# Two MLP steps on unsplit float32 operands, and pools that wait tile by tile

## The chip, the cores and the metric

The kernel runs on one core of a Trainium2 chip. The metric is the device time of one execution in microseconds (us). Times of instructions come from one execution that the hardware profiler recorded; it counts them from the start of its span.

## The reference

One layer of an encoder on x of 2048 rows by 1024, float32, in three parts: a norm and an input projection; two mixers (mLSTM heads and a Hyena convolution), whose outputs are gated, normed and go through one output projection with a norm and a residual; and an MLP. The change touches the end of the second part and the start of the third:

```
mix = concat(y_m, y_h) @ w_out                 # 2048x1024 @ 1024x1024
x   = x + rms_norm(mix, norm_mix_post)
hm  = rms_norm(x, norm_mlp_pre)
ff  = square(relu(hm @ w_mlp_in)) @ w_mlp_out  # 1024 -> 4096 -> 1024
x   = x + rms_norm(ff, norm_mlp_post)
```

## The kernel before

**Products.** Most matrix products are made of *split* operands: `split` (lines 166 and 169) rounds a tile to float32r on ScalarE (`hi`, a CAST) and subtracts it from the source on VectorE or GpSimd (`lo`). `mm3` then issues three matmuls, lo by hi, hi by lo and hi by hi (lines 159 to 161). Given an operand that is not a pair, it issues one plain float32 matmul.

**The MLP's first product** is a seven-product scheme on 2x2 blocks. Step s (0 to 31) takes 128 of 2048 paired output columns (s % 16) for one half of the rows (s // 16). `up_step` makes the products 1, 2, 6, 5, 7, 4, 3 in this order, each over k = 0 to 3 with 128x512 outputs in a bank of PSUM, and after each adds on VectorE, then relu and square on ScalarE, then stores of the results to `ga`. Product i needs a right operand `hm[i]` (1 MB, made of transposed rows and kept for sixteen steps) and a weight made by `up_weights`: two loads of 512 KB (`raw`, whose quarters are a11, a21, a12, a22), sums and differences on GpSimd (`s12`), and splits of all of it on ScalarE and GpSimd into seven tiles `cb`. `right_load` fetches an operand from DRAM (`ht`) into the space of its `lo` part, as two DMAs; `right_split` splits it in place, half by half.

**Order around step 0.** `out_proj` works through 16 blocks of 128 rows in a loop over i. For block i it transposes gated rows (`turned`), multiplies them with the output weights (`part`, four calls, into two banks `po`), and `finish` and `normed` make the residual row and its norm; `turn_out` of an earlier block transposes the normed rows and, for odd blocks, forms the seven operands on GpSimd and writes them to `ht`. In i = 11 to 14 a generator, `first_operands`, loads and splits right operands 1 and 2 and the weights of step 0. In i = 15 to 17 `first_step` runs step 0 in pieces between the last rows. In this loop the instructions of TensorE, VectorE and ScalarE keep the written order (`manual_schedule`); SP's and GpSimd's queues, and all queues in the MLP, are ordered by a planner. Banks for `po` come from a pool of three (`pp`); two more (`h1p`) serve block 1 and products 1, 2, 5 and 7 of step 0. Later steps take turns in eight banks.

**Order around step 16.** In step 15 the space of each right operand is read for the last time, and its load for the second half of the rows is issued behind that product; the split follows two products later:

```python
            if s == 15:
                self.right_load(1, i)
                loaded.append(i)
            if len(loaded) > (2 if s == 15 else 0):
                j = loaded.pop(0)
                self.right_split(j, pool if j in (2, 7, 3) else None)
```

Weights of step s + 2 are loaded, and those of s + 1 are prepared, after product 2 of step s; their raw tiles rotate through six buffers, three a step. Loads are issued from SP (line 231), most stores from ScalarE (line 234).

Of the kernel before, what the change touches and what calls it, by code (L numbers as in the profile page):

```python
# [8 lines left out]
F32 = mybir.dt.float32  # L9
F32R = mybir.dt.float32r  # L10
AF = mybir.ActivationFunctionType
ALU = mybir.AluOpType
# [135 lines left out]
class Builder:  # L148
# [95 lines left out]
    def build(self):  # L244
        tc, nc = self.tc, self.nc
        with ExitStack() as c:
            cp = c.enter_context(tc.tile_pool(name="cp", bufs=1))
# [24 lines left out]
            with ExitStack() as c2:  # L272
                self.pw = pj.enter_context(tc.tile_pool(name="pwk", bufs=2, reuse_waits="tile"))
                self.pp = pj.enter_context(tc.tile_pool(name="pps", bufs=4, space=PSUM))
# [7 lines left out]
            gp = c.enter_context(tc.tile_pool(name="gp", bufs=1, side="right"))  # L282
# [6 lines left out]
            for i, n in enumerate(("mlstm_norm_w", "hyena_norm_w")):  # L289
# [3 lines left out]
                   hy.enter_context(tc.tile_pool(name="hps", bufs=3, space=PSUM, side="right")))  # L293
# [7 lines left out]
            op = self.op = late.enter_context(tc.tile_pool(name="opre", bufs=1, side="right"))  # L301
# [3 lines left out]
            self.mtail = late.enter_context(tc.tile_pool(name="mtail", bufs=2, side="right"))  # L305
            self.mwk = ms.enter_context(tc.tile_pool(name="mwk", bufs=2, reuse_waits="tile"))
            self.mps = ms.enter_context(tc.tile_pool(name="mps", bufs=5, space=PSUM))
# [3 lines left out]
            self.h1p = c.enter_context(tc.tile_pool(name="h1p", bufs=2, space=PSUM))  # L311
            oc = ExitStack()
            self.hq = c.enter_context(tc.tile_pool(name="hmq", bufs=1))
# [6 lines left out]
            hp = c.enter_context(tc.tile_pool(name="hmp", bufs=1, side="right"))  # L320
            self.hm_pool.update({i: hp for i in (1, 2)})
            self.hm = {}
            self.cb = c.enter_context(tc.tile_pool(name="cb", bufs=1, side="right"))
# [10 lines left out]
    def long_conv(self, pools, hy, early):  # L334
# [3 lines left out]
        self.mearly = early.enter_context(self.tc.tile_pool(name="mearly", bufs=1, side="right"))  # L338
        self.mpk = early.enter_context(ExitStack())
        self.mps0 = self.mpk.enter_context(self.tc.tile_pool(name="mps0", bufs=1, space=PSUM, side="right"))  # L340
# [10 lines left out]
    def filters(self, c, consts):  # L351
        tc = self.tc
        kp = c.enter_context(tc.tile_pool(name="kp", bufs=1, side="right"))
        wk = c.enter_context(tc.tile_pool(name="kwk", bufs=2, side="right"))
        ps = c.enter_context(tc.tile_pool(name="kps", bufs=2, space=PSUM, side="right"))
        yield from self.filter_net(kp, wk, ps, consts)
        yield from self.filter_spectra(kp, wk, ps, c.enter_context(tc.tile_pool(name="kmps", bufs=1, space=PSUM, side="right")))

    def filter_loads(self, c):

        tc, io, pool = self.tc, self.io, self.pool
        kp = c.enter_context(tc.tile_pool(name="kc", bufs=1, side="right"))
# [956 lines left out]
    def out_proj(self, c):  # L1319
# [134 lines left out]
        for i in range(18):  # L1454
# [41 lines left out]
            if 10 < i < 15:  # L1496
                next(staged)
# [454 lines left out]
```

## Time and profile before

| | |
|---|---|
| time, median of 3 runs | 2719.76 us (2715.68 to 2721.2) |
| the profiled execution's own time | 2723.08 us |
| its span | 2721.3 us |
| mean granted clock of TensorE | 0.983 |
| busy: TensorE, VectorE, ScalarE, GpSimd | 96%, 56%, 45%, 45% |

PE is TensorE's matmuls, PEld its weight loads, DVE is VectorE, ACT ScalarE, POOL GpSimd, SP the engine that issues most loads; a q behind a name is the engine's queue of instructions. A matmul's record is longer than the distance to the next one, since they overlap. In rows of waits, `PE po L159 <- DVE xo` reads: TensorE's instruction of line 159 for tile po waited for VectorE's on xo. The clock is given as a share of full speed (2.4 GHz; the other level is 1.2 GHz).

### The profile page before, as it was taken

Reading aid. Unit: us, or ns where it says so; the run is one execution under the profiler, and the core shown is the slowest. Engines: PE = TensorE matmul, PEld = TensorE weight load, DVE = VectorE, ACT = ScalarE, POOL = GpSimd, SP = SyncE. Lnnn points to the kernel's source line nnn. Section 1 sums busy time; section 2 is a strip of 40 time slices with the busy share of each in tenths; the row PEclk is TensorE's granted clock in tenths of the full one; section 3 lists DMA queues with packets and bytes.
Section 4 is the critical chain, followed back from the end, with each engine's and each line's share of the span. In section 5 each row is a group of like instructions: output and inputs, shape, how many; then the busy total and the mean of one; then the engine's idle time right before and its main releaser. Section 6 shows DMA issues by size and latency. Waiting matters only on the chain.

```text
span 2721.3 us, 35529 instructions
## 1 busy us (share of the span) xinstructions
PE 2602.7 (96%) x12293; PEld 2125.3 (78%) x12293; DVE 1527.1 (56%) x2453; ACT 1237.2 (45%) x2300; POOL 1220.3 (45%) x973
## 2 busy tenths in 40 slices
PE   6999999999999998889997999989999999999998
PEld 4778888777798887767775888868888888888876
DVE  5676653777547666656455444464444433544478
ACT  6355544555544446643334454454444333222244
POOL 1211114555235443446676877677772340311232
PEclk8999999999999999989998999989999999999999
DMA  6233346665676549556755444554446453444546
GB/s 172 61 87 113 112 124 215 191 190 175 215 234 185 181 154 297 152 158 222 231 177 200 171 138 166 181 185 150 148 163 254 164 181 108 121 146 159 186 161 218
DMA packets 288355, 465.76 MB, mean 171 GB/s; under 512 B 37542, under 2 KB 149414, under 8 KB 287152
## 3 DMA queue, kind: packets, MB, share of 16 engines
q1 hardware_dynamic: 227600, 324.85, 38.3%
q10 hardware_dynamic: 53264, 117.53, 11.4%
q0 software_dynamic: 7312, 21.11, 3.1%
q8 instruction: 98, 1.61, 0.3%
q14 instruction: 81, 0.66, 0.1%
HBM read 289.27 MB, written 174.13 MB: 170 GB/s over the span
## 4 chain that ended last, share of the span: by engine, by line
PE 40%; DVE 5%; POOL 3%; DMA 3%; ACT 2%; issue 2%; ACTq 0%; DVEq 0%; POOLq 0%; SPq 0%
PE pm L160 13%; PE pm L161 13%; PE pm L159 13%; DVE cb L169 1%; POOL xt L1255 1%; DVE hm L169 1%; ACT xo L1393 1%; DMA m<-ga 1%; DVE hm L1877 0%; DMA m<-in_w_mlp_out_dram 0%; POOL cb L169 0%; DMA hm<-ht 0%; DVE xo L1396 0%; POOL ht L1428 0%; DVE hm L1807 0%
## 5 line engine op out<-in xcount | busy, mean ns | idle before, releaser
L166 ACT CAST cb<-m 128x1024 fp32r<-128x1024 f32 (+1 forms) x346 | 281.2, 847 | 442.6 <-PE pm L159 387.5
L169 DVE TENSOR_TENSOR cb<-m,cb 128x1024 fp32r<-128x1024 f32 (+1 forms) x222 | 232.5, 1084 | 306.0 <-ACT cb L166 296.3
L160 PE MATMUL pm<-hm,cb 128*128 128x512 f32 x896 | 354.6, 396 | 18.4 <-DVE hm L169 13.2
L159 PE MATMUL pm<-hm,cb 128*128 128x512 f32 x896 | 354.1, 396 | 11.1 <-POOL cb L169 6.2
L161 PE MATMUL pm<-hm,cb 128*128 128x512 f32 x896 | 352.8, 394 | 0.0
L160 PE MATMUL pm<-cb 128*128 128x512 f32 x880 | 343.4, 390 | 7.8 <-DVE cb L169 7.8
L159 PE MATMUL pm<-cb 128*128 128x512 f32 x880 | 342.3, 389 | 1.0 <-DVE cb L169 1.0
L161 PE MATMUL pm<-cb 128*128 128x512 f32 x880 | 342.5, 389 | 0.0
L169 POOL TENSOR_TENSOR cb<-m,cb 128x1024 fp32r<-128x1024 f32 x124 | 270.7, 2196 | 71.6 <-ACT cb L166 71.6
L1689 DVE TENSOR_TENSOR m<-pm,m 128x512 f32<-128x512 f32 x224 | 154.2, 690 | 250.8 <-PE pm L161 224.7
L159 PE MATMUL pt<-hn,w 128*128 128x512 f32 x640 | 270.1, 422 | 1.7 <-ACT hn L486 1.6
L160 PE MATMUL pt<-hn,w 128*128 128x512 f32 x640 | 254.2, 397 | 0.3 <-DVE hn L487 0.2
L161 PE MATMUL pt<-hn,w 128*128 128x512 f32 x640 | 253.3, 396 | 0.0
L169 POOL TENSOR_TENSOR raw<-raw,hi 128x512 fp32r<-128x512 f32 x160 | 206.1, 1300 | 100.6 <-ACT hi L166 75.4
L160 PEld LDWEIGHTS pm<-hm,cb 128*128 128x128 f32 x896 | 170.5, 190 | 59.3 <-DVE hm L169 16.6
L159 PEld LDWEIGHTS pm<-hm,cb 128*128 128x128 f32 x896 | 170.6, 190 | 51.0 <-POOL cb L169 7.9
L160 PEld LDWEIGHTS pm<-cb 128*128 128x128 f32 x880 | 165.1, 188 | 45.9 <-DVE cb L169 11.8
L161 PEld LDWEIGHTS pm<-hm,cb 128*128 128x128 f32 x896 | 170.4, 190 | 36.1
L159 PEld LDWEIGHTS pm<-cb 128*128 128x128 f32 x880 | 165.1, 188 | 35.9 <-ACT junk L1862 1.4
L161 PEld LDWEIGHTS pm<-cb 128*128 128x128 f32 x880 | 165.2, 188 | 34.0
L1693 ACT ACTIVATE m<-m 128x512 f32<-128x512 f32 x128 | 80.5, 630 | 220.4 <-DVE m L1689 213.1
L635 POOL DMA_DIRECT2D vp<-vst x96 | 61.3, 642 | 232.0 <-ACT vst L631 230.9
(322 smaller groups left out, 5672.0 us busy)
## 6 DMA issues: line engine op xcount, KB each, us to landing
ga<-m ACTq DMA_DIRECT2D x96, 512.0 KB, 4.4
m<-ga SPq DMA_DIRECT2D x96, 512.0 KB, 3.8
d<-st ACTq DMA_DIRECT2D x64, 512.0 KB, 3.0
m<-in_w_mlp_in_dram SPq DMA_DIRECT2D x62, 512.0 KB
m<-in_w_mlp_out_dram SPq DMA_DIRECT2D x114, 256.0 KB, 4.0
raw<-d SPq DMA_DIRECT2D x96, 256.0 KB, 3.2
xt<-in_x_dram SPq DMA_DIRECT2D x32, 512.0 KB, 4.0
dk<-kst SPq DMA_DIRECT2D x32, 512.0 KB, 3.8
```

Of the source, the lines that this page charges most:

```text
L159: pe.matmul(ps, w[1], x[0], start=first, stop=False)
L160: pe.matmul(ps, w[0], x[1], start=False, stop=False)
L161: pe.matmul(ps, w[0], x[0], start=False, stop=last)
L166: self.act.copy(hi, src)
L169: (eng_lo or self.dve).tensor_tensor(lo, src, hi.bitcast(F32), ALU.subtract)
L635: pool.dma_start(dst[:, 8 * b + e:8 * b + 8:2, cc:cc + 128], st[64 * e:64 * e + 64])
L1255: eng.tensor_tensor(res[:, cs], tmp[e], res[:, cs], ALU.add)
L1393: act.activation(x1, xt, AF.Square, accum_out=ss1[:, h:h + 1])
L1689: dve.tensor_tensor(dst, a, b, ALU.add)
L1693: act.activation(g, g, AF.Relu)
```

## The change

Steps 0 and 16 (the first of each half of the rows) make their products of plain float32 operands: the right operand as loaded, the weights as loaded or as summed. `up_weights(plain=True)` makes only the sums, and forms the weight of product 3 in place after product 2 has used the same space. The right operands are split behind the products: one after each later product (`split_held`), the last of them in the step that follows.

`first_operands` no longer runs in pieces: i = 11 and 12 only load operands 1 and 2, and the weights of step 0 are loaded when i = 14 ends, into a pool `m0` in place of the projection's scratch. Raw weights of step 1 go to free `cb` tiles. The norm of row 15 stands ahead of the third product of step 0. Weights of step 18 are loaded after product 3 of step 16, not after product 2.

The second output bank of each odd block up to 13 comes from `h1p`. And 25 pools are opened with `reuse_waits="tile"`: a tile in space that an earlier pool held waits for the tiles that lay there, where it waited for the release of that whole pool (`pwk`, `hwk`, `mwk`, `mmk` and some others had it already).

```diff
--- before.py
+++ after.py
-            cp = c.enter_context(tc.tile_pool(name="cp", bufs=1))
+            cp = c.enter_context(tc.tile_pool(name="cp", bufs=1, reuse_waits="tile"))
...
-            self.h1p = c.enter_context(tc.tile_pool(name="h1p", bufs=2, space=PSUM))
+            self.h1p = c.enter_context(tc.tile_pool(name="h1p", bufs=2, space=PSUM, reuse_waits="tile"))
...
-        def banks():
-            return [pp.tile([128, 512], F32, tag="po", name=f"po{e}", bufs=3) for e in range(2)]
+        def banks(i):
+
+            return [self.h1p.tile([128, 512], F32, tag="h1", name="po1") if e and i % 2 and i < 15 else
+                    pp.tile([128, 512], F32, tag="po", name=f"po{e}", bufs=3) for e in range(2)]
 
...
-        pos[0] = banks()
+        pos[0] = banks(0)
...
-        staged = self.first_operands(scratch)
-        wl = c.enter_context(tc.tile_pool(name="owl", bufs=2, side="right"))
+        wl = c.enter_context(tc.tile_pool(name="owl", bufs=2, side="right", reuse_waits="tile"))
...
-                    step = self.first_step(c, pp)
+                    step = self.first_step(pp)
                     next(step)
                     part(pos[i], 1, ym[i], 0)
                     next(step)
                     rows = finish(i, pos.pop(i))
+                    xns[i] = normed(i, *rows)
                     next(step)
-                    xns[i] = normed(i, *rows)
                 else:
                     next(step)
-            if 10 < i < 15:
-                next(staged)
+            if i in (11, 12):
+                self.right_load(0, i - 10)
             if i == 14:
                 gc.close()
+                self.first_operands(c)
             yield
         c.close()
 
...
-    def up_weights(self, s, raw, s12, pieces=False):
+    def up_weights(self, s, raw, s12, pieces=False, plain=False):
 
...
+        if plain:
+
+            pool.tensor_tensor(s12[:, 1], s12[:, 0], a11, ALU.subtract)
+            places = {1: a11, 7: a21, 2: a12, 4: a22, 5: s12[:, 0], 6: s12[:, 1], 3: a12}
+            yield lambda i, k: places[i][:, k, :]
+            pool.tensor_tensor(a12, a12, s12[:, 1], ALU.subtract)
+            yield
...
-    def first_operands(self, scratch):
-
-        for i in (1, 2):
-            self.right_load(0, i)
-        yield
-        self.right_split(1, self.pool)
-        yield
-        self.right_split(2, self.pool)
-        raw = [scratch("wr").rearrange("p (k f) -> p k f", k=4) for _ in range(2)]
-        g = self.up_weights(0, raw, scratch("ws").rearrange("p (i k f) -> p i k f", i=2, k=4))
-        next(g)
-        yield
-        self.w1_first = next(g)
-        yield
-
-    def first_step(self, c, pp):
-
-        wk = c.enter_context(self.tc.tile_pool(name="m0", bufs=1))
+    def first_operands(self, c):
+
+        m0 = self.m0 = c.enter_context(self.tc.tile_pool(name="m0", bufs=1))
+        raw = [m0.tile([128, 4, 256], F32, tag="r", name="m0", bufs=3) for _ in range(2)]
+        self.w_first = self.up_weights(0, raw, m0.tile([128, 2, 4, 128], F32, tag="r", name="m0", bufs=3), plain=True)
+        next(self.w_first)
+
+    def first_step(self, pp):
+
+
         count = [0]
+        self.held = []
 
         def tile(shape, tag):
-            return wk.tile(list(shape), F32, tag=tag, name="m0", bufs={"g": 3, "s": 1, "r": 3}[tag])
+            return self.m0.tile(list(shape), F32, tag=tag, name="m0", bufs={"g": 3, "s": 1}[tag])
 
         def bank():
             count[0] += 1
...
                 return self.h1p.tile([128, 512], F32, tag="h1", name="pm")
             return pp.tile([128, 512], F32, tag="po", name="pm", bufs=3)
 
+        def place(shape):
+            return self.cb.tile(shape, F32, tag="cb", name="m1", bufs=9)
+
+        def then(i):
+            if i != 5:
+                self.split_held()
+            self.held.append(i)
+            if i == 2:
+                next(self.w_first)
+
         for i in (6, 5):
             self.right_load(0, i)
-        nxt = self.up_weights(1, [tile((128, 4, 256), "r") for _ in range(2)], tile((128, 2, 4, 128), "r"), True)
+        w = next(self.w_first)
+        nxt = self.up_weights(1, [place([128, 4, 256]) for _ in range(2)], place([128, 2, 4, 128]), True)
         next(nxt)
         yield
         for i in (7, 4, 3):
             self.right_load(0, i)
-        products = self.up_step(0, self.w1_first, lambda: tile((128, 2, 512), "g"), lambda: tile((128, 512), "s"), bank,
-                                lambda i: None)
+        products = self.up_step(0, w, lambda: tile((128, 2, 512), "g"), lambda: tile((128, 512), "s"), bank, then, True)
         next(products)
         next(products)
-        self.right_split(6, self.pool)
-        yield
-        self.right_split(5, self.pool)
+        yield
         next(products)
         next(nxt)
         yield
-        self.right_split(7)
-        next(products)
-        self.right_split(4)
         next(products)
         next(nxt)
-        self.right_split(3)
         next(products)
+        next(products)
+        self.w1 = next(nxt)
         yield
         for _ in products:
             pass
-        self.w1 = next(nxt)
-        yield
+        yield
+
+    def split_held(self):
+        if self.held:
+            j = self.held.pop(0)
+            self.right_split(j, self.pool if j in (2, 7, 3) else None)
 
...
-            g = self.up_weights(s % 16, raw, ring((128, 2, 4, 128), 1))
+            g = self.up_weights(s % 16, raw, ring((128, 2, 4, 128), 1), plain=s == 16)
             next(g)
             return g
 
         def then(i):
-            nonlocal nxt, w1
-            if i == 2:
-                if s + 1 < n:
-                    w1 = next(nxt)
-                if s + 2 < n:
-                    nxt = weights(s + 2)
+            nonlocal nxt, w1, own
+            self.split_held()
+            if s == 16:
+                self.held.append(i)
             if s == 15:
                 self.right_load(1, i)
-                loaded.append(i)
-            if len(loaded) > (2 if s == 15 else 0):
-                j = loaded.pop(0)
-                self.right_split(j, pool if j in (2, 7, 3) else None)
+            if i == 2:
+                if s == 16:
+                    next(own)
+                if s + 1 < n:
+                    w1, own = next(nxt), nxt
+
+            if i == (3 if s == 16 else 2) and s + 2 < n:
+                nxt = weights(s + 2)
             if s == n - 1 and i in (2, 7):
                 next(down)
 
-        loaded = []
+        own = None
         w1, nxt = self.w1, weights(2)
         for s in range(1, n):
             for _ in self.up_step(s, w1, lambda: ring((128, 2, 512), 0),
-                                  lambda: self.mk.tile([128, 512], F32, tag="mc", name="m4"), next_bank, then):
+                                  lambda: self.mk.tile([128, 512], F32, tag="mc", name="m4"), next_bank, then, s == 16):
                 pass
 
-    def up_step(self, s, w, pair, single, next_bank, then):
+    def up_step(self, s, w, pair, single, next_bank, then, plain=False):
 
...
-                self.mm3(pt, w(i, k), (hi[:, k, :], lo[:, k, :]), k == 0, k == 3)
+                x = lo[:, k, :].bitcast(F32) if plain else (hi[:, k, :], lo[:, k, :])
+                self.mm3(pt, w(i, k), x, k == 0, k == 3)
```

## Rows read from the trace of the kernel before

**Rows 1.** The page, part 1: busy us, share of the span, instructions.

```profile
PE 2602.7 (96%) x12293; PEld 2125.3 (78%) x12293; DVE 1527.1 (56%) x2453; ACT 1237.2 (45%) x2300; POOL 1220.3 (45%) x973
```

**Rows 2.** Busy time by stretch (from:to, length, engines; clock, DMA share, GB/s).

```profile
1163.00:1214.00 51.00, 42.58 (x178) 30.58 (x177) 31.01 (x53) 25.36 (x52) 23.68 (x18) 0.90 0.53 165
1330.00:1431.90 101.90, 92.65 (x419) 71.64 (x418) 52.55 (x87) 39.25 (x88) 76.79 (x64) 0.97 0.64 203
1431.90:1474.70 42.80, 27.63 (x101) 20.00 (x99) 29.70 (x27) 18.35 (x28) 24.75 (x17) 0.84 0.52 192
1600.00:1619.10 19.10, 19.10 (x86) 15.74 (x85) 8.83 (x12) 9.00 (x13) 13.86 (x8) 1.00 0.46 160
1763.90:1807.00 43.10, 31.90 (x107) 22.98 (x106) 33.99 (x27) 26.51 (x36) 32.66 (x15) 0.84 0.54 205
```

**Rows 3.** ScalarE's timeline, copies of product 1, steps 6, 15 and 19.

```profile
1577.08 0.59 ACT L1702 COPY m<-pm 128x512 f32<-128x512 f32 x1 [0.71 <-PE pm L161]
...
1749.22 0.59 ACT L1702 COPY m<-pm 128x512 f32<-128x512 f32 x1 [0.72 <-PE pm L161]
...
1844.80 0.59 ACT L1702 COPY m<-pm 128x512 f32<-128x512 f32 x1 [0.71 <-PE pm L161]
```

**Rows 4.** TensorE's timeline where step 0 begins.

```profile
1428.14 1.17 PE L1406 MATMUL pto<-eye,xo 128*128 128x128 f32 x8
...
1431.93 0.39 PE L159 MATMUL pm<-hm,cb 128*128 128x512 f32 x1
...
1434.65 0.39 PE L159 MATMUL pm<-hm,cb 128*128 128x512 f32 x1
```

**Rows 5.** Waits in step 0 (us in total, times, longest).

```profile
PE pm L160 <- DVE hm L169: 9.1, 4, 3.8
```

**Rows 6.** Waits in steps 16 and 17.

```profile
PE pm L160 <- DVE hm L169: 4.1, 3, 2.7
...
PE pm L160 <- POOL hm L169: 3.4, 2, 1.8
```

**Rows 7.** Waits at the projection's end, 1330 to 1432 us.

```profile
PE po L159 <- DVE xo L1254: 4.0, 3, 2.3
...
PE py L1290 <- DVE xo L1407: 2.1, 2, 1.8
...
PE ptp L1306 <- POOL ymt L1300: 2.1, 1, 2.1
```

**Rows 8.** TensorE's timeline around a plain product.

```profile
540.77 1.02 PE L1177 MATMUL pi<-z,ci 128*128 128x512 f32 x2
...
541.86 0.40 PE L160 MATMUL pt<-hn,w 128*128 128x512 f32 x1
```

**Rows 9.** Groups on GpSimd, 1330 to 1432 us (busy us, mean ns | idle before).

```profile
L169 POOL TENSOR_TENSOR cb<-wr,cb 128x1024 fp32r<-128x1024 f32 (+1 forms) x3 | 6.7, 2237 | 0.0
...
L169 POOL TENSOR_TENSOR hm<-hm,hm 128x1024 fp32r<-128x1024 f32 x2 | 5.1, 2558 | 5.2 <-ACT hm L166 5.2
```

**Rows 10.** Instructions on tile hm (ns min/median/max; first, last start us).

```profile
L169 DVE TENSOR_TENSOR hm<-hm,hm x21: 1210/1329/3768, 1333.8 to 1796.6; 128x1024 fp32r<-128x1024 f32 x21
...
DMA to landing us min/median/max: 3.5/7.0/11.3
```

**Rows 11.** SP's queue: issue start us, us, in the second seam.

```profile
1745.53 10.49 SPq L231 DMA_DIRECT2D m<-in_w_mlp_in_dram  x2
1756.11 15.54 SPq L231 DMA_DIRECT2D hm<-ht  x14
```

**Rows 12.** VectorE's timeline in row 15's finish.

```profile
1440.11 3.55 DVE L1250 TENSOR_TENSOR ps<-pss 128x1 f32<-128x1 f32 x1
...
1446.88 1.98 DVE L1255 TENSOR_TENSOR xt<-xo,xt 128x512 f32<-128x512 f32 x1
```

**Rows 13.** Groups on VectorE, steps 16 and 17.

```profile
L169 DVE TENSOR_TENSOR hm<-hm,hm 128x1024 fp32r<-128x1024 f32 x11 | 20.1, 1844 | 9.7 <-ACT hm L166 9.7
```

**Rows 14.** Waits over the whole span.

```profile
PEld pt L160 <- issue: 14.9, 62, 0.2
```

More of the change, by code (lines that the diff above doesn't have):

```diff
@@ L273, in build @@
                 self.pw = pj.enter_context(tc.tile_pool(name="pwk", bufs=2, reuse_waits="tile"))
-                self.pp = pj.enter_context(tc.tile_pool(name="pps", bufs=4, space=PSUM))
+                self.pp = pj.enter_context(tc.tile_pool(name="pps", bufs=4, space=PSUM, reuse_waits="tile"))
                 work = self.project()
@@ L281, in build @@
             self.gates_done = False
-            gp = c.enter_context(tc.tile_pool(name="gp", bufs=1, side="right"))
+            gp = c.enter_context(tc.tile_pool(name="gp", bufs=1, side="right", reuse_waits="tile"))
             self.qt = gp.tile([128, 4, 128], F32, name="qt")
@@ L292, in build @@
             hyp = (hy.enter_context(tc.tile_pool(name="hwk", bufs=2, side="right", reuse_waits="tile")),
-                   hy.enter_context(tc.tile_pool(name="hps", bufs=3, space=PSUM, side="right")))
+                   hy.enter_context(tc.tile_pool(name="hps", bufs=3, space=PSUM, side="right", reuse_waits="tile")))
             with tc.manual_schedule():
@@ L299, in build @@
             hs.close()
-            op = self.op = late.enter_context(tc.tile_pool(name="opre", bufs=1, side="right"))
+            op = self.op = late.enter_context(tc.tile_pool(name="opre", bufs=1, side="right", reuse_waits="tile"))
             self.ahead = {k: op.tile([128, D], F32, name=f"wf{k}") for k in range(4, 8)}
@@ L304, in build @@
             self.ahead["y"] = [op.tile([128, 4, 128], F32R, name=f"y0{e}") for e in range(2)]
-            self.mtail = late.enter_context(tc.tile_pool(name="mtail", bufs=2, side="right"))
+            self.mtail = late.enter_context(tc.tile_pool(name="mtail", bufs=2, side="right", reuse_waits="tile"))
             self.mwk = ms.enter_context(tc.tile_pool(name="mwk", bufs=2, reuse_waits="tile"))
-            self.mps = ms.enter_context(tc.tile_pool(name="mps", bufs=5, space=PSUM))
+            self.mps = ms.enter_context(tc.tile_pool(name="mps", bufs=5, space=PSUM, reuse_waits="tile"))
             self.mlstm()
@@ L492, in normalise @@
         act, dve = self.act, self.dve
-        wk = c.enter_context(tc.tile_pool(name="nwk", bufs=2))
-        ps = c.enter_context(tc.tile_pool(name="nps", bufs=3, space=PSUM, side="right"))
+        wk = c.enter_context(tc.tile_pool(name="nwk", bufs=2, reuse_waits="tile"))
+        ps = c.enter_context(tc.tile_pool(name="nps", bufs=3, space=PSUM, side="right", reuse_waits="tile"))
         xs = {}
@@ L1441, in out_proj @@
         yz[1] = turned(zs.pop(1), 1, 0)
-        pos[1] = [pp.tile([128, 512], F32, tag="po", name="po0", bufs=3), self.h1p.tile([128, 512], F32, tag="h1", name="po1")]
+        pos[1] = banks(1)
         part(pos[1], 0, yz[1], 4)
```

30 lines of the change are left out of this document (15 added, 15 removed).

## Prediction

> **What bounds the kernel now.** I read the page's shares first: TensorE is counted busy 96% of the span [rows 1]. So time is won only where TensorE stands still, runs at the lower clock, or does less. The busy time of stretches shows where that is. A steady step of the MLP (1600 to 1619.1 us) is busy all the time at full clock. Three stretches around the change are not: the end of the output projection (1330 to 1431.9), step 0 of the MLP's first product (1431.9 to 1474.7: 27.6 of 42.8 us busy, clock 0.84), and steps 16 and 17 (31.9 of 43.1 us, 0.84) [rows 2]. A record of TensorE overlaps the next one, so idle time is understated there; the loss is better taken from start to start.
>
> For that I use ScalarE's copy of a step's product 1. Nine steady steps from 1577.08 to 1749.22 take 19.13 us each. From step 15's copy to step 19's it is 1844.80 - 1749.22 = 95.58 us where four steps need 76.52: **19.1 us are lost at the second seam** [rows 3]. Step 0's first matmul starts at 1431.93, step 6's copy at 1577.08: 145.15 us [rows 3, 4]. Six steps (114.8), one product (twelve matmuls from 1431.93 to 1434.65, 2.72 us [rows 4]; 2.9 with the copy's delay) and sixteen transposes (eight take 0.9 to 1.17 us [rows 4]; 1.8) need 119.5: **25.6 us are lost at the first seam**. In the 101.9 us ahead of it TensorE idles 9.3 us at a mean clock of 0.97 [rows 2]; with some work done at half clock I count 10.8.
>
> Who ends these waits? In step 0 above all VectorE's splits of the right operands (9.1 us) [rows 5]; in steps 16 and 17 the splits on VectorE and GpSimd (4.1 and 3.4) [rows 6]; ahead of step 0 an output bank that VectorE frees late (4.0), and gate rows that GpSimd and VectorE finish late (2.1 and 2.1) [rows 7]. The diff touches all of them.
>
> **The change, part by part.** *Plain products.* A split product is three matmuls per k, 0.227 us apart: 0.68 us [rows 4]. The trace has plain float32 matmuls of the same 128x512 shape: one instruction of line 1177 leaves two records, and from its start to the matmul after next, with one split matmul between, it is 541.86 - 540.77 = 1.09 us; less 0.23, a plain one takes 0.86 us [rows 8]. Steps 0 and 16 have 28 each: 28 x (0.86 - 0.68) = **+5.0 us per step, +9.9 in all**, on TensorE and hidden by nothing. A plain step is 24.1 us.
>
> *No splits ahead of step 0.* Out of the projection's end go the splits of operands 1 and 2 and of the first weights: on GpSimd 6.7 + 5.1 us in that stretch [rows 9], besides sums and the casts on ScalarE. GpSimd is busy 76.8 of 101.9 us there [rows 2] and makes the gates and residual rows that TensorE waits for. The bank from the other pool takes away two of the three bank waits, 4.0 in all; the third and longest, 2.3 us, I take for row 15's, which keeps its pool [rows 7]. Bounds: 2 us back (bank alone) to 10.8 (all). I take **-8**, near the upper one, since splits stand in the chain ahead of most of these waits.
>
> *Step 0.* Its products wait for landed data, not for casts and subtractions. The loads of operands 6 and 5 keep their place behind the output weights whose space they take. Ahead of product 6 come three sums on GpSimd (1.3 us each, an estimate: half a split's 2.6 of [rows 9], for half the width) in place of a whole preparation. Of the 25.6 something stays, since VectorE and ScalarE run in written order here. From product 1's start, plain product 1 ends at 3.4, 2 at 6.9. Then come the split of operand 1 on VectorE (two of 1.2 to 3.8 us [rows 10]), row 15's finish (8.8 us now, of which one tiny addition is 3.6 [rows 12]; some 6) and its norm, some 2: so the adds of product 6 come at 15 to 20. They free product 2's bank, which product 7 wants at 14.7: 3 us of waiting. The norm, moved ahead, is ready before row 15's transposes. Step 1's product 6 may wait 2 us for the weights' sums, whose cast stands behind product 4's squares and operand 5's casts, and I allow 3 for step 1's products 7 and 4, whose splits come last. Step 2's weights can be loaded when product 3 of step 0 ends. So 8 us stay (bounds 2 and 20): -25.6 + 5.0 + 8 = **-12.6**.
>
> *Steps 16 and 17.* Today the right operands' loads stand in SP's queue behind a weight load that waits until 1756, though product 1 of step 15 is copied at 1749.2 [rows 3, 11]. In the change that weight load (for step 18) goes into space that step 16 uses to its end, so it must come behind all fourteen. Then a load can start with each product that step 15 ends, the last near 1766; they took 15.5 us to issue and 7 to land, median [rows 10, 11], so the last are in at about 1773. Plain product 3 starts 20.7 us into step 16, near 1786. TensorE runs through. What must be ready 24.1 us later? GpSimd has a steady step's 13.9 us [rows 2], the late subtraction (1.3) and two splits of 2.6: 20.4. VectorE has ten splits at 1.84 [rows 13] and a steady step's 8.8 [rows 2]: 27.2, so 3 us spill into step 17, where they are needed some 13 us in; eight banks let the adds lag. Step 18's weights load only when step 16 ends: 5 us to land (an estimate inside the 3.5 to 11.3 of [rows 10]) and 14 to prepare make 19 against the 19.1 of step 17, and product 1 needs only the first part. I leave 2.5 us (bounds 0 and 14): -19.1 + 5.0 + 2.5 = **-11.6**.
>
> *Waits by tile.* A tile of a new pool waits for the tiles that it replaces, not for the whole pool. From 1163 to 1214, where the output projection takes over, TensorE idles 8.4 us [rows 2]; its first weights may be made earlier. Between -5 and, if the queues not ordered by hand come out otherwise, +4; I take **-1**. In the long stretches full TensorE hides it.
>
> **Sum:** -8 - 12.6 - 11.6 - 1 = -33.2 us against the profiled execution's own 2723.1 us (span 2721.3): 2689.9. That execution was 3.3 us above the median of 2719.76; against the median it is 2686.6, say 2687.
>
> *A rule that speaks against it.* VectorE's splits of one form take from 1.21 to 3.77 us [rows 10]; eleven in 1763 to 1807 took 20.1 [rows 13]. The Trainium skill, page SBUF — State Buffer, section Who interferes with whom, says that a VectorE instruction with two SBUF inputs contends with a GpSimd instruction that reads SBUF. The spread of durations agrees with it. If nearly every split meets GpSimd, the time is that of the first rival; by the mean it is the sum above.
>
> **Rivals.** *VectorE becomes the bound* (chance 0.15). Both seams put some ten splits beside a GpSimd that is nearly full. At 3.3 us each, near the top of [rows 10], step 16 asks for 33 + 8.8 and step 17 for 3.3 + 8.8: 54 us where TensorE needs 43.2. Then 11 us stand at each seam in place of the 2.5 and 8: -33.2 + 8.5 + 3 = -21.7, 2698; up to 10 more if GpSimd, held up in turn, also keeps the delays ahead of step 0: 2708. For it: the 3.77. Against: the mean of 1.84.
>
> *More instructions for more waits: slower* (0.07). TensorE's weight loads of line 160 already stood 62 times for 0.24 us (14.9 in all) behind an instruction of their own queue [rows 14]. If finer waits turn one wait into several, each costs that much where TensorE is the bound. To eat 33 us and 5.4 more takes 160 of them; 200 give 2687 + 48 = 2735. Against: in the long stretches tiles replace tiles of their own pool, and the other waits are at borders of pools.
>
> *The change gives nothing* (0.05). The waits move by one step, to steps 1 and 17, at today's price, and the 8 us ahead of step 0 pay most of the 9.9: 2717 to 2724. For it: the splits are nearly as many as before. Against: each has 24 us more.
>
> *Waits by tile free more* (0.03): with all of the 8.4 and as much at the kernel's start and other borders, -17 more, 2670 or below.
>
> **Numbers.** The forecast has 0.70; half way to its bounds it is 2672 to 2700. With the other cases 2670 to 2710 leaves out the slower, the unchanged and the lowest case, 0.15. A measurement of this kernel tells about 0.2%, 5.4 us, from no change. Faster 0.88, within it 0.05, slower 0.07.
>
> **What would show it.** Two records per k in steps 0 and 16 and some 24 us for the products of each without long gaps; product-1 copies of steps 15 and 19 some 84 us apart; no split of a right operand before step 0; right loads issued from the copy of step 15 on. I am wrong if TensorE waits in steps 1 and 17 as it does now in 0 and 16, if sums on GpSimd come after product 6 is due, or if stretches far from the seams change.

## The result

The kernel after takes 2703.07 us (median of 6 runs, 2699.94 to 2707.6), the kernel before on the same chip 2717.57 (2713.51 to 2721.2): a ratio of 0.9947 [0.9934, 0.996], faster by 14.5 us. The forecast was 2687, its range 2670 to 2710. So the sign and the range held, and less than half of the 33.2 us came. A second comparison, below, gives the same ratio, 0.9948 [0.9935, 0.996].

The profiled execution has a span of 2698.5 us, 22.8 below that of before. TensorE's busy time fell by 4.1 us [rows 1]:

```profile
PE 2598.6 (96%) x12237; PEld 2109.2 (78%) x12237; DVE 1541.0 (57%) x2454; ACT 1230.1 (46%) x2292; POOL 1206.1 (45%) x964
```

Busy time by stretch, for [rows 2]: the projection's end, step 0, the 42 us behind it, a steady step, and the second seam. Columns: from:to, length, busy time and instructions of PE, PEld, DVE, ACT and POOL, granted clock, DMA share, GB/s.

```profile
1330.00:1416.46 86.46, 84.03 (x391) 66.48 (x391) 49.10 (x77) 28.55 (x72) 57.98 (x53) 0.98 0.65 211
1416.46:1452.98 36.52, 26.40 (x74) 12.08 (x72) 24.93 (x27) 18.03 (x27) 25.61 (x16) 0.96 0.67 249
1452.98:1495.00 42.02, 34.65 (x120) 26.88 (x121) 26.10 (x19) 17.17 (x24) 35.99 (x24) 0.83 0.48 169
1600.00:1619.10 19.10, 19.10 (x85) 15.77 (x84) 8.49 (x11) 8.97 (x14) 14.34 (x9) 1.00 0.45 152
1719.30:1762.40 43.10, 43.10 (x175) 32.56 (x175) 22.03 (x24) 21.89 (x31) 29.29 (x16) 1.00 0.72 253
```

The reader is to see three things. The projection's end has 2.4 us of idle time left, where it had 9.3. Step 0 takes 36.5 us in place of 42.8, though 26 would do (24.1 and sixteen transposes). And the 42 us behind it, step 1 and most of step 2, are now a seam of their own: 7.4 us idle and a clock of 0.83. In the kernel before, the 42 us behind step 0 had 3.1 us idle at the full clock:

```profile
1474.70:1516.70 42.00, 38.87 (x168) 31.46 (x169) 18.59 (x21) 17.29 (x25) 35.65 (x24) 1.00 0.57 186
```

The copies of product 1 on ScalarE for steps 6, 15, 19 and 22 [rows 3]:

```profile
1566.31 0.59 ACT L1717 COPY m<-pm 128x512 f32<-128x512 f32 x1 [0.71 <-PE pm L161]
...
1744.70 0.57 ACT L1717 COPY m<-pm 128x512 f32<-128x512 f32 x1
...
1823.99 0.57 ACT L1717 COPY m<-pm 128x512 f32<-128x512 f32 x1
...
1878.98 0.59 ACT L1717 COPY m<-pm 128x512 f32<-128x512 f32 x1 [0.71 <-PE pm L161]
```

The copies of steps 15 and 19 carry no idle time: ScalarE was late with them (at step 15 behind a cast that waited 6.1 us for GpSimd's subtraction), and TensorE was not. So the marks 15 and 19, which the forecast used, don't measure the second seam here; steps 6 and 22 do, where the copy waits for TensorE on both sides. From one to the other it is 312.67 us; before it was 325.10 (step 22's copy at 1902.18, three steady steps behind step 19's in [rows 3]). The second seam gave 12.4 us.

Now all stretches between such marks in order, from the traces of before and of the kernel after in both comparisons, in us:

| stretch | before | after, first | after, second | forecast |
|---|---|---|---|---|
| to the projection's first matmul | 1178.97 | 1172.32 | 1177.42 | -1 (waits by tile) |
| from there to step 0's first matmul | 252.96 | 244.14 | 243.38 | -8 |
| to the copy of step 6 | 145.15 | 149.85 | 153.84 | -12.6 |
| to the copy of step 14 | 153.01 | 153.01 | 153.01 | 0 |
| to the copy of step 22 | 172.09 | 159.66 | 160.10 | -11.6 |
| rest | 819.11 | 819.55 | 818.59 | 0 |

Two terms came as forecast (-8.8 and -9.6; -12.4 and -12.0). One has the wrong sign: from step 0 to step 6's copy the kernel after is slower by 4.7 and 8.7 us. That is 17 to 21 us short of the forecast for this stretch; the whole shortfall is 33.2 - 14.5 = 18.7.

Where it goes shows in TensorE's waits of the kernel after, first from 1416 to 1500 us, then from 1719 to 1880 (total, times, longest) [rows 5, 6]:

```profile
PE pm L159 <- DVE m L1703: 6.4, 1, 6.4
PE pm L159 <- POOL cb L169: 4.9, 2, 3.2
PE pto L1408 <- DVE xo L1398: 2.8, 1, 2.8
PE pm L160 <- POOL hm L169: 2.5, 1, 2.5
...
PE pm L159 <- POOL cb L169: 1.0, 2, 0.7
```

VectorE's splits, 9.1 us of waits in step 0 before, are gone from the list. In their place step 1's first matmul waits 6.4 us for an *addition* of step 0 that frees its bank, row 15's transposes wait 2.8 us for its norm, and step 2 waits 4.9 us for its weights. From step 0's first matmul to step 6's copy such waits add up to 18.3 us before and to 17.5 and 19.5 in the two traces of the kernel after: the change moved them and hardly took any away, and the plain products' 5.0 us came on top. That TensorE waits in step 1 as it did in step 0 is one of the signs of being wrong that the prediction named.

ScalarE's timeline says why the norm is late:

```profile
1424.11 0.29 ACT L239 ACTIVATE po_sd<-ps,eps 128x1 f32<-128x1 f32 x1 [0.39 <-DVE ps L1250]
1430.45 1.04 ACT L166 CAST hm<-hm 128x1024 fp32r<-128x1024 f32 x1 [6.04 <-DMA hm<-ht]
...
1431.40 1.05 ACT L1395 ACTIVATE xo<-xt 128x1024 f32<-128x1024 f32 x1
1432.36 0.19 ACT L1395 ACTIVATION_READ_ACCUMULATOR xo<-xt 128x1 f32 x1
1432.57 0.29 ACT L1396 ACTIVATE ss<-ss,eps 128x1 f32<-128x1 f32 x1
```

The squares of row 15 (line 1395) stand behind a cast that sat 6.04 us until an operand landed; the row itself was ready 3.3 us before they start (line 1255 ends on VectorE at 1428.05). By the order of the program's instructions the cast is that of operand 4, which VectorE's timeline below bears out. The code calls that split in step 1, behind product 1. The planner had put it, and the casts of operand 3 behind it, into step 0, ahead of the casts of operands 2, 6, 5 and 7. On VectorE:

```profile
1433.10 0.75 DVE L1398 TENSOR_SCALAR xo<-xt,r 128x1024 f32<-128x1024 f32 x1
1433.77 0.68 DVE L1703 TENSOR_TENSOR m<-pm,m 128x512 f32<-128x512 f32 x1
...
1441.46 1.38 DVE L169 TENSOR_TENSOR hm<-hm,hm 128x1024 fp32r<-128x1024 f32 x1 [0.30 <-PE pm L157]
1443.18 8.45 DVE L169 TENSOR_TENSOR hm<-hm,hm 128x1024 fp32r<-128x1024 f32 x3 [0.34 <-PE pm L157]
1451.55 1.28 DVE L1703 TENSOR_TENSOR m<-pm,m 128x512 f32<-128x512 f32 x2
```

Four splits (operand 4's two, then operand 6's two) stand ahead of the last two additions from banks of step 0 (1451.55). The first two start, at 1441.46 and 1443.18, 0.3 us after TensorE has read the halves of operand 4: products 7, 4 and 3 run from 1436.01 with 0.43 us a record, so product 4's halves end near 1441.2 and 1442.9. On TensorE, step 0's first matmul and step 1's:

```profile
1416.46 10.46 PE L157 MATMUL pm<-hm,m 128*128 128x512 f32 x24
...
1452.98 0.77 PE L159 MATMUL pm<-hm,cb 128*128 128x512 f32 x1 [6.40 <-DVE m L1703]
```

Step 1's first matmul starts 0.15 us after the second of those additions ends; that it waits for the bank is read from this, since all else that it needs was ready earlier.

### The profile page after: what moved, and what is told of

It is laid out like the page before. It is cut to its first block, busy times and chain, and to the rows that moved or that the text cites. A ratio compares the mean times of both kernels' runs of the same rounds, so it can differ in the third digit from the quotient of the medians.

```text
span 2698.5 us, 35390 instructions
## 1 busy us (share of the span) xinstructions
PE 2598.6 (96%) x12237; PEld 2109.2 (78%) x12237; DVE 1541.0 (57%) x2454; ACT 1230.1 (46%) x2292; POOL 1206.1 (45%) x964
## 4 chain that ended last, share of the span: by engine, by line
PE 39%; DVE 4%; POOL 4%; issue 3%; DMA 2%; ACT 2%; ACTq 0%; DVEq 0%; SPq 0%; POOLq 0%
PE pm L159 13%; PE pm L160 13%; PE pm L161 13%; DMA m<-in_w_mlp_out_dram 1%; POOL xt L1255 1%; DVE cb L169 1%; POOL cb L169 1%; ACT xo L1395 1%; DVE hm L1892 0%; DVE hm L169 0%; DVE xo L1398 0%; DMA hm<-ht 0%; DVE gss L1297 0%; POOL ht L1430 0%; DVE hm L1822 0%
## 5 line engine op out<-in xcount | busy, mean ns | idle before, releaser
L159 PE MATMUL pm<-hm,cb 128*128 128x512 f32 x840 | 331.4, 394 | 12.3 <-DVE m L1703 6.4
L160 PE MATMUL pm<-hm,cb 128*128 128x512 f32 x840 | 330.2, 393 | 2.5 <-POOL hm L169 2.5
L161 PE MATMUL pm<-hm,cb 128*128 128x512 f32 x840 | 329.7, 393 | 0.0
L159 PEld LDWEIGHTS pm<-hm,cb 128*128 128x128 f32 x840 | 159.2, 189 | 49.0 <-POOL cb L169 7.6
L159 PEld LDWEIGHTS pm<-cb 128*128 128x128 f32 x880 | 165.1, 188 | 36.5 <-ACT junk L1877 1.4
L160 PEld LDWEIGHTS pm<-hm,cb 128*128 128x128 f32 x840 | 159.4, 190 | 37.4 <-POOL hm L169 2.9
L161 PEld LDWEIGHTS pm<-hm,cb 128*128 128x128 f32 x840 | 159.2, 190 | 34.2
```

Source lines behind the costliest of these rows:

```text
L159: pe.matmul(ps, w[1], x[0], start=first, stop=False)
L160: pe.matmul(ps, w[0], x[1], start=False, stop=False)
L161: pe.matmul(ps, w[0], x[0], start=False, stop=last)
```

## The experiments

**Which part gave what.** Four kernels take the change apart: the 25 waits by tile alone, everything but these, the first seam alone and the second alone (the last two with the waits by tile).

```diff
# t_before_tile: the kernel before, and in 25 places as here
-            cp = c.enter_context(tc.tile_pool(name="cp", bufs=1))
+            cp = c.enter_context(tc.tile_pool(name="cp", bufs=1, reuse_waits="tile"))
# t_after_notile: the kernel after, these 25 back
# t_seam1: the kernel after, and in up()
-            g = self.up_weights(s % 16, raw, ring((128, 2, 4, 128), 1), plain=s == 16)
+            g = self.up_weights(s % 16, raw, ring((128, 2, 4, 128), 1))
...
-                                  ..., next_bank, then, s == 16):
+                                  ..., next_bank, then):
# with then() and its list of loaded operands from the kernel before
# t_seam2: the kernel before with the 25, and up_weights(), up(), up_step() of after
```

> The kernel before with the 25 waits by tile alone; nothing else of the change. The traces of before and after stand 6.7 us apart where the output projection's first matmul starts (1178.97 and 1172.32), ahead of every other edit. Theory (the prediction's term): waits by tile give 1 us, and the rest of the 6.7 is the spread from run to run; then this kernel is 0 to 3 us faster than before, ratio 0.999 to 1.000. Rival: the waits by tile give the 6.7 us themselves; ratio 0.997 to 0.998, and the projection's first matmul starts near 1172 in its trace. Third: they cost time in the stretches after it (more waits on TensorE's queue), so that 6.7 won there is given back: the first matmul near 1172, the whole at a ratio of 0.999 to 1.001.

> The kernel after without the 25 waits by tile; all else of the change stands. By the prediction's term (1 us) the time is that of the kernel after plus 1, a ratio of 0.994 to 0.996 to before. If the waits by tile gave 6.7 us, it is 0.996 to 0.998. If they cost time, or made the planner's order in step 0 worse, it is under 0.993.

> The kernel after, but the second row's first step (step 16) as before: split operands, loads and splits where they were. By the traces the second seam gave 12.4 us (forecast 11.6), so this kernel should lose that against the kernel after: a ratio of 0.999 to 1.000 to before if the whole gain after the start of step 0 is the second seam's, and copies of product 1 of steps 15 and 19 95 us apart again. Rival: the second seam's gain depends on what the first left (weights and rings shifted), then the ratio stays under 0.997.

> The kernel before with the waits by tile and with step 16 plain alone; step 0 and the end of the output projection as before. By the forecast's terms -11.6 - 1: a ratio of 0.995 to 0.996. If the first seam as a whole gives nothing (step 0 gained 6.3 us and steps 1 to 5 gave back 11 in the traces, against 8.8 won ahead of step 0), this kernel is as fast as the kernel after, 0.994 to 0.996; if the first seam gave what its marks show (4 us in all), 0.996 to 0.997.

Measured, as ratios to the kernel before on that chip (median 2722.26 us): waits by tile alone 0.9984 [0.9974, 0.9993]; all but these 0.9945 [0.9932, 0.9957]; first seam 0.9969 [0.9957, 0.9981]; second seam 0.9938 [0.9926, 0.9951].

The second seam with the waits by tile is as fast as the whole change (0.9947 and 0.9948). Against the waits by tile alone it gives 2717.7 - 2707.53 = 10.2 us by medians; the first seam, that carried two thirds of the forecast, gives 2717.7 - 2715.4 = 2.3, and here the two intervals overlap. In the trace of the first seam alone the projection's end is 243.35 us and the stretch to step 6's copy 152.41: of the 9.6 us won ahead of step 0, 7.3 are given back behind it, as in the kernel after. The first seam alone was expected at 0.999 to 1.000 and came out lower, under 0.997 as by the rival that the second seam's gain depends on the first. But the second seam alone has that gain too: 313.11 us from step 6's copy to step 22's.

The waits by tile are worth 2 to 7 us by the first of these ratios, which lies between what the term and its rival had it at, and nothing that can be measured by the second (0.9945 against 0.9947 with them). One wait shows in the traces. In the kernel before and in t_after_notile the mLSTM's first transposes wait 1.5 and 1.6 us for a load of k behind the Hyena stage; with the waits by tile they don't. From the last matmul of that stage's tile pi to the first of these transposes (tile ptk) it is 9.23 and 9.35 us without them, 7.61 to 7.63 in the twelve traces with them. The first matmul of the projection lies at 1172.0 to 1178.1 us in these twelve and at 1178.97 and 1179.44 in the two without. The same kernel's two traces lie 5.1 us apart there, so of the 6.7 us in the table at most a part is the change's.

**Is it the order?** If the pulled-up splits are the cause, holding step 1 to its written order must bring the time back. The second edit also makes one block of the projection's last three rounds, so that row 15's transposes come where they are written. The third moves the norm back to its place in the kernel before.

```diff
# g1_step1_order: the kernel after, in up()
         for s in range(1, n):
-            for _ in self.up_step(...):
-                pass
+            with ExitStack() as order:
+                if s == 1:
+                    order.enter_context(self.tc.manual_schedule(engines={...PE, ...DVE, ...Activation}))
+                for _ in self.up_step(...):
+                    pass
# g3_both: this, and in out_proj()
+        tail = ExitStack()
         for i in range(18):
-            with tc.manual_schedule(engines={...}):
+            if i == 15:
+                tail.enter_context(tc.manual_schedule(engines={...}))
+            with ExitStack() as order:
+                if i < 15:
+                    order.enter_context(tc.manual_schedule(engines={...}))
# n_norm_late: the kernel after, in out_proj()
                     rows = finish(i, pos.pop(i))
-                    xns[i] = normed(i, *rows)
                     next(step)
+                    xns[i] = normed(i, *rows)
```

> The kernel after itself, run beside the three others, so that they are compared with it on one chip. Expected as before: a ratio of 0.993 to 0.996; from step 0's first matmul to the copy of product 1 of step 6 it takes 150 to 155 us, where the kernel before takes 145 to 146.

> The kernel after, with step 1 of the MLP in a block of its own whose order is as written on TensorE, VectorE and ScalarE, so that the splits of operands 4 and 3, written in step 1, can't be put into step 0. In the kernel after the planner had put their casts ahead of row 15's norm on ScalarE (a wait of 6.0 us for operand 4's landing) and operand 4's two subtractions ahead of the last adds of step 0 on VectorE. Theory (order): this is what ate the first seam's gain; row 15's norm comes some 5 us earlier, the last adds of step 0 some 5 us earlier, step 1's first matmul waits 0 to 2 us in place of 6.4 to 7.3, and the kernel is 5 to 9 us faster than the kernel after: ratio 0.990 to 0.993, step 0's first matmul to step 6's copy 142 to 147 us. Rival (VectorE and GpSimd are full): the same splits come later and step 1 waits for them instead; within 2 us of the kernel after, and gaps of over 2 us ahead of step 1's products 4 and 3.

> As the run before, and also the projection's last three rounds in one block, so that row 15's transposes stand behind step 0's product 4, as written, in place of ahead of product 7. Theory (order): the wait of 2.8 to 5 us for row 15's norm ahead of its transposes goes as well; 1 to 4 us faster than with step 1's block alone: ratio 0.989 to 0.992. Rival: product 7 waits for the same adds, which stand behind the norm on VectorE in either order; no difference (within 2 us) to the run before.

> The kernel after with row 15's norm written behind step 0's third product again, as in the kernel before. With this the adds of product 6 stand ahead of the norm on VectorE. If the change was right to put the norm ahead, this is 2 to 5 us slower than the kernel after (its transposes wait longer). If the norm ahead is what holds up the adds and the bank of product 7, it is 1 to 4 us faster. By the forecast the transposes would wait for the norm: slower.

Measured: the kernel after 0.9948 [0.9935, 0.996], 2706.61 us; step 1 in written order **0.9906 [0.9892, 0.9919], 2695.83 us**; both blocks 0.9918 [0.9904, 0.9931]; the norm late 0.9946 [0.9932, 0.996].

Holding step 1 to its written order is worth 10.8 us by medians. The block fixes the order of all of step 1; that the splits of operands 4 and 3 carry the gain is read from the trace. ScalarE's timeline of g1_step1_order, where the cast stood:

```profile
1423.82 0.29 ACT L239 ACTIVATE po_sd<-ps,eps 128x1 f32<-128x1 f32 x1 [0.68 <-DVE ps L1250]
...
1427.91 1.06 ACT L1395 ACTIVATE xo<-xt 128x1024 f32<-128x1024 f32 x1 [3.80 <-DVE xt L1255]
```

The squares now wait for their own row and for nothing else. The last additions of step 0 and step 1's first matmul:

```profile
1444.87 1.28 DVE L1706 TENSOR_TENSOR m<-pm,m 128x512 f32<-128x512 f32 x2
...
1446.30 0.77 PE L159 MATMUL pm<-hm,cb 128*128 128x512 f32 x1 [3.16 <-DVE m L1706]
```

Counted from step 0's first matmul (1415.86) the squares start at 12.1 us in place of 14.9, the last additions of step 0 at 29.0 in place of 35.1, and step 1's first matmul at 30.4 in place of 36.5. From there to step 6's copy it takes 112.0 us (113.3 before the edit): step 1 doesn't pay it back. From step 0's first matmul to step 6's copy: 142.39 us. TensorE's waits from 1416 to 1500:

```profile
PE pm L160 <- DVE hm L169: 4.3, 4, 1.7
PE pm L159 <- DVE m L1706: 3.2, 1, 3.2
PE pm L160 <- POOL hm L169: 2.0, 1, 2.0
PE pm L159 <- ACT hm L166: 1.3, 1, 1.3
PE pm L157 <- DVE m L1706: 0.9, 1, 0.9
```

Step 1's first matmul waits 3.2 us, where 0 to 2 were expected. Step 2's wait for weights (4.9) is gone from the list: SP's load of them waits for step 0's last subtraction on VectorE (line 1743 there, 1746 here), which lets it go 42.8 us after step 0's first matmul in place of 48.9. The rival was right about one thing: step 1 now waits 4.3 us for splits of its operands, four times. It was not enough to undo the gain.

The other two gave nothing. Both blocks are 2.2 us slower than step 1's alone by medians (2698.05 us), with intervals that overlap, where 1 to 4 us faster were expected. The transposes' wait is gone, as expected, but step 1's first matmul waits 9.9 us (TensorE, 1417.8 to 1510 us):

```profile
PE pm L159 <- DVE m L1712: 9.9, 1, 9.9
...
```

In written order the split of operand 5 and the copies of row 15's transposed rows (line 1409) stand on VectorE ahead of step 0's last addition. So the planner did no harm that can be measured by moving row 15's transposes ahead of product 7; moving operand 4's splits was the harm. The norm late changes nothing: the transposes wait 4.1 us for it in place of 2.8, and step 1's first matmul 5.3 in place of 6.4. The last additions of step 0 don't come earlier for it (35.7 us after step 0's first matmul, in place of 35.1); TensorE only gets to that wait later.

**What is left?** Of the forecast's stretch from the projection to step 6's copy (398.11 - 8 - 12.6 = 377.5 us) the run above leaves 384.4 - 377.5 = 6.9 us missing (9.3 in the second trace of that kernel, g1_again). Two runs shift splits of the first row between VectorE and GpSimd, and one undoes the bank.

```diff
# c1_vector_only, c2_more_gpsimd: g1_step1_order, and in split_held()
-            self.right_split(j, self.pool if j in (2, 7, 3) else None)
+            self.right_split(j, self.pool if j in (() if self.first else (2, 7, 3)) else None)
# c2: ((2, 6, 5, 7, 4, 3) if self.first else (2, 7, 3))
# first_step() sets self.first = True, step 15 sets it False
# b_bank: the kernel after, in banks()
-            return [self.h1p.tile(...) if e and i % 2 and i < 15 else
+            return [self.h1p.tile(...) if e and i == 1 else
```

> The kernel with step 1 in written order again, as the base of the next two on the same chip: 0.989 to 0.992 of before, as measured.

> The kernel with step 1 in written order, and of the first row's right operands (steps 0 and 1) VectorE makes all splits; GpSimd, which made the second half of operands 2, 7 and 3, makes none. What is left at the first seam after the order is mended is 6.9 us against the forecast of 377 us from the projection's first matmul to step 6's copy (384.4 measured). Theory (the two engines hold each other up): three splits fewer of 2.5 to 2.7 us on GpSimd, VectorE gets three of 1.2 but its others no longer stretch (one took 7.9 us, four 2.3 to 3.4, beside GpSimd); step 1's waits for splits (7.6 us in the trace) halve: 2 to 5 us faster than the base. Rival (VectorE's queue alone is the limit): three more splits make its adds and splits later, 2 to 4 us slower. Neither counts: within 1.5 us.

> The counterpart: GpSimd makes the second half of operands 2, 6, 5, 7, 4 and 3 in steps 0 and 1, three halves more than the base. Theory (the two engines hold each other up, and GpSimd has the next weights to prepare): VectorE's remaining splits stretch as much, and weights for step 2 come 7 to 8 us later; 4 to 9 us slower than the base. Rival (VectorE's queue alone is the limit): it is relieved of three splits, 2 to 4 us faster.

> The kernel after (planner's order left as it was) without the bank more: the second half of odd rows 3 to 13 takes its bank from the projection's own pool again, as in the kernel before; row 1 keeps the other pool's. By the forecast's bounds the bank alone was worth 2 us ahead of step 0, most of two bank waits of 4.0 us in all; so 2 to 4 us slower than the kernel after (ratio 0.995 to 0.997), with two waits of some 2 us for VectorE's rows between 1330 and 1415 us besides row 15's. If the earlier splits had set those waits, it is no slower and the waits are gone without the bank.

Measured: the base 0.9913 [0.9899, 0.9927], 2697.8 us; VectorE alone **0.9893 [0.9879, 0.9906], 2691.58 us**; more on GpSimd 0.9917 [0.9903, 0.993], 2697.29 us; the kernel after without the bank 0.9951 [0.9938, 0.9963].

VectorE alone is 6.2 us faster by medians, 29 us faster than the kernel before, and the fastest kernel here; from step 0 to step 6's copy it takes 138.88 us. But not for the reason that I gave. TensorE's waits from step 0 to 1510 us, the base first, then VectorE alone, then more on GpSimd:

```profile
PE pm L160 <- DVE hm L169: 3.4, 3, 1.5
PE pm L159 <- DVE m L1706: 3.2, 1, 3.2
PE pm L159 <- POOL cb L169: 2.9, 2, 1.9
PE pm L159 <- ACT hm L166: 1.4, 1, 1.4
PE pm L160 <- POOL hm L169: 1.3, 1, 1.3
...
```

```profile
PE pm L160 <- DVE hm L169: 5.4, 5, 1.7
PE pm L159 <- DVE m L1707: 3.2, 1, 3.2
PE pm L159 <- ACT hm L166: 1.1, 1, 1.1
...
```

```profile
PE pm L159 <- POOL cb L169: 8.3, 5, 4.5
PE pm L160 <- POOL hm L169: 5.4, 1, 5.4
...
```

With VectorE alone the waits for GpSimd (2.9, both in step 1, and 1.3) are gone and those for VectorE's splits have grown from 3.4 to 5.4. VectorE's splits, the base first (shortest, median, longest in ns):

```profile
L169 DVE TENSOR_TENSOR hm<-hm,hm x11: 1218/1656/4069, 1426.5 to 1476.7; 128x1024 fp32r<-128x1024 f32 x11
```

```profile
L169 DVE TENSOR_TENSOR hm<-hm,hm x14: 1212/1574/3395, 1423.5 to 1473.1; 128x1024 fp32r<-128x1024 f32 x14
```

They got little shorter, though I had expected it: by 0.08 us in the median. By these waits the part that comes back is GpSimd's own queue: it prepares the next weights, and three splits of 2.5 to 3.4 us stood between them. With three halves more on GpSimd VectorE's eight splits shrink to a median of 1.25 us, and TensorE waits 13.7 us for GpSimd, none for VectorE's splits; the time is that of the base, where 4 to 9 us slower were expected. Which rival holds depends on the direction: taking work off GpSimd pays, taking it off VectorE doesn't.

The bank more gives nothing that can be measured, where 2 to 4 us were expected. Without it TensorE waits for the bank 2.9 us in two places from 1330 us to step 0, with it 2.3 in one; before it was 4.0 in three [rows 7]:

```profile
PE po L159 <- DVE xo L1254: 2.9, 2, 2.2
```

## Why the prediction was half right

**Plain products** (+5.0 us per step): holds. Step 16's 56 records stand 0.429 us apart from 1754.64 to 1778.24 us without a gap, so one of the 28 takes 0.858 us, and the step 24.0.

**The projection's end** (-8): measured -8.8 and -9.6. By elimination the larger part is what was named, the splits and weights taken out: without the bank the stretch takes 244.5 us, without the waits by tile 242.6, much as with them. GpSimd is busy 58.0 of 86.5 us, where it was 76.8 of 101.9 [rows 2]; that its relief counts, and not ScalarE's (28.6 of 86.5 us, where it was 39.3 of 101.9), no run separates. The bank's share, 2 us at least by my lower bound, was too high: without it, too, only 0.6 us of the two other waits for banks is left. Row 15's wait stayed, 2.3 us, as forecast.

**The second seam** (-11.6): measured -12.4 and -12.0. SP's queue in the trace of after, for [rows 11]:

```profile
1738.22 19.38 SPq L231 DMA_DIRECT2D hm<-ht  x14
1757.70 0.49 SPq L231 DMA_DIRECT2D m<-in_w_mlp_in_dram  x1
```

The loads of the right operands begin as step 15's product 1 ends (1738.22) and are issued 19.4 us later, with the weight load behind them; the forecast had 17 for the same (1749 to 1766). VectorE's eleven splits took 24.2 us, not 20, and hardly a wait followed (1.0 us for weights): by the forecast's account the eight banks and 24 us of plain products cover it, which no run tests by itself. Of the 19.1 us 1.7 and 2.1 stay besides the 5.0, where the forecast had 2.5. One of the signs that I named there was badly chosen, the distance of the copies of steps 15 and 19: 79.3 us, not 84, because ScalarE was late with the first one.

**Step 0: the step that failed** is the residual of 8 us (bounds 2 and 20) in the term -25.6 + 5.0 + 8, and in it the sentence "VectorE and ScalarE run in written order here". The seam's products need 119.5 + 5.0 = 124.5 us; measured are 149.85 and 153.84, a residual of 25.3 and 29.3, beyond my bound. Written order holds inside a block. The splits of operands 4 and 3 had been moved by the change out of step 0's blocks into step 1, which has none, and nothing kept them behind step 0. I had gone through what stands ahead of the adds of product 6 (finish, norm, split of operand 1) and had not asked where the two splits could go that no longer belonged to a block. For the same reason the norm, moved ahead, was not "ready before row 15's transposes": they wait 2.8 us for it. With the two splits held in their place, the residual is 142.39 - 124.5 = 17.9 and 19.1, inside the bounds but near the upper one. With the splits off GpSimd it is 14.4. So the order is the largest part of the miss, 10.8 us by medians of the 17 to 21, and 6.4 us above the forecast's 8 stay even in the fastest kernel.

Of the further parts of the residual, one is named by c1_vector_only: GpSimd's queue, which I had costed only for step 16. Another stays there and in both traces with step 1 in order: 3.2 us ahead of step 1's first matmul for step 0's last additions, and 3.4 to 5.4 for splits in step 1. I had 3 us for products 7 and 4 of step 1 and 3 for product 7's bank in step 0 (0.9 measured); the bank of step 1's first product I had not looked at. A third part has no term at all in the 8 us: time at the lower clock. From step 0's first matmul to step 6's copy the granted clock was 0.95 before; in the kernel after, in g1_step1_order and in c1_vector_only it is

```profile
1416.46:1566.31 149.85, 132.36 (x506) 97.72 (x505) 81.18 (x86) 70.72 (x101) 116.17 (x70) 0.94 0.50 176
```

```profile
1415.86:1558.25 142.39, 130.53 (x506) 94.88 (x505) 83.28 (x87) 69.84 (x101) 117.94 (x71) 0.96 0.53 189
```

```profile
1418.34:1557.22 138.88, 128.15 (x506) 94.28 (x505) 81.89 (x89) 69.94 (x102) 110.28 (x67) 0.99 0.53 188
```

Behind the wait of 6.4 us in the kernel after, step 1's matmuls first stand 0.43 us apart (1453.54, 1453.97, 1454.39), the pace of 1.2 GHz, and 0.23 from 1457.28 on. So that wait cost more than its own length; how much of the residual this is in all, no run separates.

The range had a slip in its working: half way from 2687 to the bounds of the four terms is 2679 to 2704, not 2672 to 2700 (2672 is the full lower bound). The measured 2703 lies outside the one and just inside the other.

**VectorE becomes the bound** (0.15, 2698 to 2708): the time fell into this rival's range, but its mechanism is not the main one. Its splits did stretch (8.45 us for three), yet the written order and the splits taken off GpSimd bring the time to 2691.58 us while VectorE has three splits more. **More instructions for more waits** and **nothing** fell. **Waits by tile**: -1 with bounds of -5 and +4 stands; between 0 and 7 by two comparisons that don't agree well, and only 1.5 us of it is located.

## What to carry to other kernels

When an edit takes work out of a block whose order is fixed, ask where the planner may put it, on each engine: an instruction that waits for a late load, pulled up in an in-order queue, holds everything that stands behind it there. Read a seam's end not by who waited before the edit but by the last instruction that frees the next stage's banks and buffers, here two additions behind four splits. And before halving work between two engines, see what else the slower one must deliver in that stretch.

## What the chip showed that I had not expected

A VectorE split of 128x1024 takes 1.21 us at its shortest [rows 10]. In g1_step1_order one took 7.89:

```profile
1462.98 7.89 DVE L169 TENSOR_TENSOR hm<-hm,hm 128x1024 fp32r<-128x1024 f32 x1 [0.90 <-ACT hm L166]
```

From 1463.51 to 1472.01 GpSimd ran two splits and two sums without a pause longer than 0.1 us:

```profile
1463.51 5.05 POOL L169 TENSOR_TENSOR hm<-hm,hm 128x1024 fp32r<-128x1024 f32 x2
1468.18 1.59 POOL L1527 TENSOR_TENSOR m<-m 128x512 f32<-128x512 f32 x1
1469.85 2.16 POOL L1528 TENSOR_TENSOR m<-m 128x512 f32<-128x512 f32 x1
```

So the price of such a meeting isn't bounded by the 3.77 us of [rows 10]: by these times one instruction of VectorE was held through three of GpSimd's. It is seen once at this length; in the other trace of the same kernel, g1_again, the same split took 4.07. The Trainium skill, page SBUF — State Buffer, section Who interferes with whom, says that a VectorE instruction with two SBUF inputs contends with a GpSimd instruction that reads SBUF, and that issue order decides who blocks. The trace agrees with the first: nearly all of the cost fell on VectorE here (GpSimd's splits took 2.7, where 2.5 is usual). It doesn't bear out the second, as far as recorded starts tell the order of issue: VectorE's split starts at 1462.98, 0.53 us ahead of GpSimd's first, and is the one that was held.
